# Attention's transposes in unbroken groups, the planner's TensorE spacing, and where attention's output is prepared

## The chip, the cores and the metric

The kernel runs on one core of a Trainium2 chip. The metric is the device time of one execution in microseconds; where several runs are shown, their median counts. The engines are named as the profile names them: PE is TensorE (PEld its weight loads), DVE is VectorE, ACT is ScalarE, POOL is GpSimd, SP is the engine that issues the DMAs.

## The reference

One decoder block on 1024 tokens of width 1024. Half of the mixing width (8 heads of 64) is stick-breaking attention, the other half (4 heads of 128) is a gated DeltaNet in chunks.

```python
h = rmsnorm(x, norm1_w);  proj = h @ w_in
# attention, strictly causal, per head
z = q @ k.T / sqrt(64)
sp = where(causal, softplus(z), 0)
tail = cumsum(sp, reverse=True) - sp
attn = where(causal, exp(log_sigmoid(z) - tail), 0)
o_sb = rmsnorm(attn @ v, sb_norm_w) * silu(sb_z)
# DeltaNet: causal conv + silu on q, k, v, l2norm, chunked delta rule with decay
o_gdn = rmsnorm(gated_delta(q, k, v, decay, beta), gdn_norm_w) * silu(g_z)
x = x + concatenate([o_sb, o_gdn]) @ w_out
return rmsnorm(x, final_norm_w)
```

## The kernel before

Everything is float32. A product that needs full precision is split: each operand into a high part in the format fp32r and a low part, and three matmuls (`mm3`: high x high, high x low, low x high) stand for one. A column of the input projection is 128 outputs wide and takes eight steps (k) of three 512-column matmuls for each half of the tokens. Its weights arrive as `wer`, ScalarE copies them to the high part `weh`, and GpSimd subtracts for the low part `wel` (`Columns.split`, two halves of four k each). The column being computed asks for the split of the next column at its 8th and 12th step.

The program is recorded through a planner. `Model` has a cost for each instruction and keeps a clock; `interleave` runs generators ("streams") and, whenever TensorE's queue in the model is empty, lets the ready stream of the smallest number record its next piece. TensorE's instructions stand in the order in which they were recorded. On the other engines (V, A, G and S for the DMAs) an instruction joins a heap when its inputs are done by the model's clock, and the heap's smallest priority (`ck.prio`, which is a stream's third argument) goes next; this order is then fixed by dependencies. So a cost in the model moves instructions on every engine.

The streams: the DeltaNet ones (load, substitute, solve, pre, scan) come first. Attention follows: `attention` opens a `window` for each head and each quarter of the queries. A window computes scores `z`, two sigmoids, a product scan `cc`, and multiplies them on GpSimd into `sg`. Then it transposes the weights (`st` is the same memory read as fp32r; the profile calls it `stf`) in groups of three or four 128x128 blocks into one PSUM tile, splits that into `ah` and `al`, and multiplies with the values into `po`. At its end it turns two blocks `ot`. `projections` (the columns) is the stream that fills TensorE's gaps. When it is used up, `products_delta` and `products_attention` do so: they multiply the mixed outputs with `w_out`, eight blocks of tokens each, two halves of 12 matmuls per block.

Ahead of the products, `enter_delta` and `enter_attention` load a block `mx` and normalise it, and `prepare` calls `split`, which turns its four 128x128 blocks (plain fp32), multiplies with the gate into `mf`, and makes `mh` (ScalarE) and `ml` (GpSimd). The products' sums are added to the residual `xr` on VectorE; in the last half of each block follow the square sums `sy` (through `yj`), `ry`, the scaling with `fnw` and the write to `out`. `turned` is the helper that records a group of transposes; a yielded `GAP` lets any other ready stream go before this one continues. `ORDER` of the columns, pools and buffer counts are not touched.

All recorded instructions have the line of the recording helper, L360, so the profile tells them apart by the names of their tiles.

Of the kernel before, what the change touches and what calls it, by code (L numbers as in the profile page):

```python
# [11 lines left out]
F32R = mybir.dt.float32r  # L12
I32 = mybir.dt.int32
AF = mybir.ActivationFunctionType
ALU = mybir.AluOpType
# [20 lines left out]
OUT_WEIGHTS, DELTA, WEIGHTS, BANK, WINDOW, OUTPUT, RESULT, DECAYS = -1, 0, 2, 5, 10, 12, 20, 25  # L36
# [6 lines left out]
GAP = "gap"  # L43
# [122 lines left out]
class Model:  # L166
# [3 lines left out]
    def __init__(self, engines):  # L170
        self.now, self.events, self.seq = 0.0, [], 0
        self.regions = {}
        self.heads = {e: [] for e in "VAGS"}
        self.busy = {e: False for e in "VAGS"}
        self.order = {e: [] for e in "VAGS"}
        self.pe, self.pe_busy, self.pe_began, self.table, self.dma = [], False, 0.0, None, 0.0
        self.prio, self.pe_rows, self.pe_words = 0, 128, False

        self.held = {"V": 0.0, "G": 0.0}
        for e, real in engines.items():  # L180
            setattr(self, e, Recorder(self, e, real))
# [18 lines left out]
    def record(self, eng, ins, outs, inputs, cost, table):  # L200
        self.seq += 1
        op = Op(eng, ins, cost, self.prio, self.seq, table)
        if eng == "P":
            op.rows = rows(inputs[0])
            op.words = cost == 58
            op.load = int(np.prod(inputs[0].shape[1:])) * (0.445 if inputs[0].dtype == F32R else 0.834)
        deps = {}
        for ap in outs + inputs:
            r = self.regions.get(ap.tensor.name)
# [112 lines left out]
    def pull(self):  # L322
        if self.pe and not self.pe_busy and not self.pe[0].waits:
            op = self.pe[0]
            self.pe_busy = True
            self.begin(op)
            at = max(self.now, op.ready, self.pe_began + op.load)
            self.pe_began = at

            if op.words and self.pe_words:  # L330
                at += 27
            self.pe_words = op.words
            if op.rows != self.pe_rows:
                at += 150
                self.pe_rows = op.rows
            self.at(at + op.cost, self.pe_done)
# [139 lines left out]
def block(tc, xT_d, x_d, n1_d, wE_d, wQ_d, wC_d, conv_d, alog_d, dtb_d, mixw_d, wo_d, fnw_d, out_d):  # L476
    nc = tc.nc
    ck = Model({"V": nc.vector, "A": nc.scalar, "G": nc.gpsimd, "P": nc.tensor, "S": nc.sync})
    V, A, G, TE, S = ck.V, ck.A, ck.G, ck.P, ck.S

    with ExitStack() as top:
# [69 lines left out]
        def turned(tp, parts):  # L551
            ck.hold(tp)
            for u, a in enumerate(parts):
                if u:
                    yield GAP
                if a.dtype == F32R:
                    TE.transpose(tp[:, u * P:(u + 1) * P].bitcast(F32R), a, idr)
                else:
                    TE.transpose(tp[:, u * P:(u + 1) * P], a, ident)
            ck.free(tp)  # L560

        class Columns:

# [855 lines left out]
        def prepare(g):  # L1419
            for b in range(NB):  # L1420
                yield lambda: ("in", b, g) in ready and (b < 3 or f"{'ad'[g]}{b - 3}" in flags) and (b > 2 or g or f"d{5 + b}" in flags)
                mx, gt, xr, r = ready["in", b, g]
                if g == 0:
                    xr = ready[b, 1][3]
                yield r
                yield lambda: ps.room("pz", 4)
                ready[b, g] = *(yield from split(pools[0], mx, gt)), xr
                yield
# [32 lines left out]
        def enter_attention():  # L1461
            yield lambda: "pool1" in flags and "z3" in flags and 3 in wts
            f0, f1 = pools[0], pools[1]
            for b in range(NB):
                yield lambda: f"e{SBH - 1}{b // 2}" in flags and (b < 3 or (b - 3, 0) in ready)
                mx = f1.tile([P, 512], F32, tag="mx", bufs=3, name="mx")
                gt = f1.tile([P, 4, P], F32, tag="gt", bufs=3, name="gt")
                S.dma_start(mx, o_s[b])
                ck.hold(mx, gt)
                S.dma_start(gt, gate_s[0:4, :, b * P:(b + 1) * P].rearrange("k e t -> e k t"))  # L1470
                o = mx.rearrange("p (h d) -> p h d", d=SBD)
                sq = f0.tile([P, 512], F32, tag="sq", name="sq")
                G.tensor_tensor(sq, mx, mx, ALU.mult)
                ss = f0.tile([P, SBH], F32, tag="ssb", name="ssb")
                V.tensor_reduce(ss, sq.rearrange("p (h d) -> p h d", d=SBD), AX.X, ALU.add)
                rs = f0.tile([P, SBH], F32, tag="rsb", name="rsb")
                V.tensor_scalar(ss, ss, 1.0 / SBD, EPS, ALU.mult, ALU.add)
                rsqrt(rs, ss, SBH)
                ready["in", b, 0] = mx, gt, None, V.tensor_tensor(o, o, rs.unsqueeze(2).to_broadcast([P, SBH, SBD]), ALU.mult)
                yield  # L1480

        def products_attention():
            yield lambda: f"d{NB - 1}" in flags
            for b in range(NB):
# [3 lines left out]
                for got in product(b, 0, parts):  # L1488
# [37 lines left out]
                   [Stream(delta_scan(), 0, DELTA), Stream(delta_solve(), 0.5, DELTA + 0.5), Stream(delta_substitute(), 0.6, DELTA + 0.6),  # L1526
                    pre, Stream(delta_load(), 0.4, DELTA + 0.4), Stream(attention(), 9.995, WINDOW), Stream(attention_values(), 9.99, WINDOW), Stream(out_weights(), 9, OUT_WEIGHTS), fill,
                    Stream(enter_delta(), 9.3, OUTPUT), Stream(prepare(1), 9.2, OUTPUT), Stream(products_delta(), 101, OUTPUT),
                    Stream(enter_attention(), 9.1, OUTPUT), Stream(prepare(0), 9.05, OUTPUT - 1), Stream(products_attention(), 102, OUTPUT - 1.5)])

        order = mybir.DependencyInfo(mybir.DependencyClass.NoSync, mybir.DependencyReason.DATA)
        for ops in ck.order.values():
# [35 lines left out]
```

## Time and profile before

| | us |
|---|---|
| median of 3 runs | 660.68 (659.98 to 661.3) |
| the profiled execution's own time | 661.59 |
| its span | 659.87 |
| TensorE busy in it | 647.9 |
| VectorE, ScalarE, GpSimd busy | 453.9, 382.6, 343.6 |

The span runs from the first to the last instruction. Busy time of TensorE counts from a matmul's start to a modelled end, and neighbouring matmuls overlap, so the distance from start to start is the better measure of what one costs.

### The profile page before, as it was taken

What the parts mean: (1) busy time and instruction counts of PE and PEld (TensorE: products, weight loads), DVE (VectorE), ACT (ScalarE), POOL (GpSimd) and SP (SyncE); (2) the same over time, 40 slices, a digit from 0 to 9 for tenths busy, and PEclk for the clock granted to TensorE, in tenths of its full rate; (3) what the DMA queues carried; (4) which work ended last, traced back from release to release, by engine and by line L of the source; (5) the groups of instructions that cost most, each with busy time, mean ns of one, the idle gap of its engine ahead of it and who ended that gap; (6) DMA issues with size and microseconds to landing.
All of it is one profiled execution on the core that took longest, in us unless ns stands there. A gap on an engine that the chain in (4) does not pass through costs nothing.

```text
span 659.9 us, 11679 instructions
## 1 busy us (share of the span) xinstructions
PE 647.9 (98%) x3978; PEld 553.6 (84%) x3978; DVE 453.9 (69%) x851; ACT 382.6 (58%) x913; POOL 343.6 (52%) x372
## 2 busy tenths in 40 slices
PE   8999999999999999999998999999999999999996
PEld 7889888988878888888887888889888888888885
DVE  4358984434465868776887686775856867868874
ACT  6645567834546776677774576755767577311322
POOL 0106144928674867457858574632533454156753
PEclk9999999999999999999998999999999999999998
DMA  8929336863683353535387253351446916663322
GB/s 297 332 95 364 112 128 224 306 203 112 211 255 134 94 175 110 162 99 180 104 231 230 83 192 100 81 172 61 133 151 198 344 45 224 233 187 96 128 96 96
DMA packets 97643, 111.83 MB, mean 169 GB/s; under 512 B 29552, under 2 KB 62512, under 8 KB 97584
## 3 DMA queue, kind: packets, MB, share of 16 engines
q1 hardware_dynamic: 97584, 111.09, 52.0%
q8 instruction: 31, 0.51, 0.3%
q14 instruction: 28, 0.23, 0.1%
HBM read 76.03 MB, written 35.03 MB: 168 GB/s over the span
## 4 chain that ended last, share of the span: by engine, by line
PE 79%; DMA 8%; DVE 5%; POOL 4%; issue 2%; ACT 1%; SPq 0%; POOLq 0%; ACTq 0%
PE pp L360 50%; PE pz L360 22%; PE po L360 6%; PE pc L360 2%; DMA xr<-xT 2%; DVE xl L360 2%; POOL tt L360 2%; DVE xr L360 2%; DMA rs_s<-rstd 2%; DMA conv<-conv 1%; DMA xr<-x 1%; DMA wcr<-wC 1%; DMA wer<-wE 1%; POOL wel L360 1%; SPq L360 0%
## 5 line engine op out<-in xcount | busy, mean ns | idle before, releaser
L360 PE MATMUL pp<-xh,weh 128*128 128x512 f32 x360 | 152.0, 422 | 0.0
L360 PE MATMUL pp<-xh,wel 128*128 128x512 f32 x360 | 142.0, 395 | 2.4 <-POOL wel L360 2.4
L360 PE MATMUL pp<-xl,weh 128*128 128x512 f32 x360 | 141.6, 393 | 0.5 <-DVE xl L360 0.3
L360 POOL TENSOR_TENSOR sgf<-sgf,cc 128x128 f32<-128x128 f32 (+3 forms) x64 | 79.2, 1238 | 89.6 <-DVE cc L360 61.7
L360 POOL TENSOR_TENSOR wel<-wer,weh 128x512 fp32r<-128x512 f32 x48 | 62.8, 1311 | 51.6 <-ACT weh L360 45.6
L360 PEld LDWEIGHTS pp<-xh,wel 128*128 128x128 f32 x360 | 67.8, 188 | 18.5 <-POOL wel L360 3.2
L360 PEld LDWEIGHTS pp<-xh,weh 128*128 128x128 f32 x360 | 67.8, 188 | 9.7
L360 PEld LDWEIGHTS pp<-xl,weh 128*128 128x128 f32 x360 | 68.2, 189 | 8.7 <-DVE xl L360 1.3
L360 DVE TENSOR_TENSOR al<-pz,ah 128x512 fp32r<-128x512 f32 (+1 forms) x80 | 50.5, 633 | 24.9 <-ACT ah L360 24.4
L360 ACT ACTIVATE sgf<-pz,rs 128x384 f32<-128x384 f32 (+3 forms) x96 | 54.4, 588 | 22.4 <-PE pz L360 21.9
L360 ACT ACTIVATE ah<-pz 128x512 fp32r<-128x512 f32 (+1 forms) x80 | 44.5, 557 | 37.8 <-PE pz L360 37.7
L360 PE MATMUL pz<-step,stf 128*128 128x128 f32 x288 | 60.7, 247 | 0.0
L360 DVE TENSOR_TENSOR_SCAN cc<-pz,step 128x384 f32<-128x384 f32 (+2 forms) x64 | 54.0, 849 | 9.1 <-ACT pz L360 8.5
L360 PE MATMUL pp<-woh,mh 128*128 128x512 f32 (+2 forms) x132 | 52.9, 401 | 0.2 <-DVE xr L360 0.2
L360 ACT ACTIVATE pz<-pz,ns 128x384 f32<-128x384 f32 (+3 forms) x96 | 52.4, 565 | 0.0
L360 PE MATMUL pp<-woh,ml 128*128 128x512 f32 (+2 forms) x132 | 50.9, 385 | 0.0
L360 PE MATMUL pp<-wol,mh 128*128 128x512 f32 (+2 forms) x132 | 50.7, 384 | 0.0
L360 POOL TENSOR_TENSOR ac<-ac,pre 128x512 f32<-128x512 f32 x24 | 31.0, 1290 | 33.5 <-ACT pre L360 16.9
L360 DVE SCALAR_TENSOR_TENSOR pp<-pre,conv,pp 128x512 f32<-128x512 f32 x42 | 31.5, 751 | 23.5 <-ACT pp L360 22.9
L360 PEld LDWEIGHTS pz<-step,stf 128*128 128x128 f32 x288 | 38.8, 141 | 5.8 <-issue 0.2
L360 PE MATMUL po<-ah,v2a 128*128 128x256 f32 (+1 forms) x160 | 42.8, 290 | 0.0
L360 DVE TENSOR_TENSOR_SCAN cc<-pz,cc,step 128x512 f32<-128x512 f32 (+1 forms) x32 | 38.8, 1213 | 4.3 <-ACT pz L360 3.2
(266 smaller groups left out, 1613.2 us busy)
## 6 DMA issues: line engine op xcount, KB each, us to landing
wer<-wE SPq DMA_DIRECT2D x48, 256.0 KB, 3.6
xr<-x SPq DMA_DIRECT2D x16, 512.0 KB, 7.4
g_s<-ac SPq DMA_DIRECT2D x24, 256.0 KB, 2.5
v_s<-v2e SPq DMA_DIRECT2D x16, 256.0 KB, 2.8
kq<-g_s SPq DMA_DIRECT2D x16, 256.0 KB, 4.6
v2a<-v_s SPq DMA_DIRECT2D x8, 512.0 KB, 4.3
q<-qk_s SPq DMA_DIRECT2D x8, 512.0 KB, 3.9
kh<-qk_s SPq DMA_DIRECT2D x8, 512.0 KB, 4.8
```

Source lines behind the costliest of these rows:

```text
L360: ins = f(*args, **kw).ins
```

## The change

The helper `turned` no longer yields between the transposes of a group, so they are recorded one right behind the other. In the model, the extra 27 ns between two transposes of fp32r data are gone; instead the least distance from the start before it (`op.load`) is 0.665 ns per column for such a transpose (85 ns for 128) and 0.845 for any other matmul's weights (108 ns), where it was 0.445 for all fp32r operands (57 ns) and 0.834 for others. The squares of attention's output block go from GpSimd to ScalarE. `enter_attention` gets the priority 9 (OUTPUT - 3) in place of 12 on the queues of V, A, G and S, and `prepare(0)` gets 10 in place of 11; `products_attention` stays at 10.5.

```diff
-            op.words = cost == 58
-            op.load = int(np.prod(inputs[0].shape[1:])) * (0.445 if inputs[0].dtype == F32R else 0.834)
+            op.load = int(np.prod(inputs[0].shape[1:])) * (0.665 if cost == 58 else 0.845)
...
             at = max(self.now, op.ready, self.pe_began + op.load)
             self.pe_began = at
-
-            if op.words and self.pe_words:
-                at += 27
-            self.pe_words = op.words
...
             for u, a in enumerate(parts):
-                if u:
-                    yield GAP
                 if a.dtype == F32R:
                     TE.transpose(tp[:, u * P:(u + 1) * P].bitcast(F32R), a, idr)
                 else:
                     TE.transpose(tp[:, u * P:(u + 1) * P], a, ident)
             ck.free(tp)
+            yield from ()
...
                 sq = f0.tile([P, 512], F32, tag="sq", name="sq")
-                G.tensor_tensor(sq, mx, mx, ALU.mult)
+                A.activation(sq, mx, AF.Square)
...
-                    Stream(enter_attention(), 9.1, OUTPUT), Stream(prepare(0), 9.05, OUTPUT - 1), Stream(products_attention(), 102, OUTPUT - 1.5)])
+                    Stream(enter_attention(), 9.1, OUTPUT - 3), Stream(prepare(0), 9.05, OUTPUT - 2), Stream(products_attention(), 102, OUTPUT - 1.5)])
```

What this moves is shown at three places. The first is TensorE at the first transposes of head 0's last window (15 blocks in four groups); `weh`, `wel` and `pp` belong to a column, `xct`, `v`, `kn`, `at` to the DeltaNet. Before:

```order
L360 MATMUL pz<-step,stf_2684 128x128
L360 MATMUL pp<-xh,weh 128x512
L360 MATMUL pp<-xl,weh 128x512
L360 MATMUL pp<-xh,wel 128x512
L360 MATMUL pc<-xct,xinv 128x128
L360 MATMUL pz<-step,stf_2684 128x128
L360 MATMUL pp<-xh,weh 128x512
L360 MATMUL pp<-xl,weh 128x512
L360 MATMUL pp<-xh,wel 128x512
```

Now, for the same window:

```order
L355 MATMUL pp<-xh,wel 128x512
L355 MATMUL pz<-v_2620,kn 128x128
L355 MATMUL pz<-vr,at 128x128
L355 MATMUL pz<-step,stf_2643 128x128 x8
L355 MATMUL pp<-xh,weh 128x512
L355 MATMUL pp<-xl,weh 128x512
L355 MATMUL pp<-xh,wel 128x512
L355 MATMUL pc<-state,kq 128x128
L355 MATMUL pp<-xh,weh 128x512
L355 MATMUL pp<-xl,weh 128x512
```

Two groups of four stand behind each other as eight transposes, where single ones alternated with a step of a column. Over the whole order, the 384 transposes of fp32r data (`stf`, `otf`, `vt`) form 251 unbroken runs before and 104 now.

The second place is GpSimd around the low weights of the sixteenth column (k3), beside the DeltaNet's third head: `tt` are products of its block solve, `kq` its scaled queries, `sgf` attention's product of sigmoid and scan, `ac` a gate of the convolution. Before:

```order
L360 TENSOR_TENSOR sgf_4045<-sgf_4045,cc 128x896
L360 TENSOR_TENSOR kq<-kq,cb 128x4x128
L360 TENSOR_TENSOR tt<-xa,nb 128x512 x2
L360 TENSOR_TENSOR tt<-yx,xb 128x512 x2
L360 TENSOR_TENSOR wel<-wer,weh 128x512
L360 TENSOR_TENSOR rr<-ss,half 128x8
L360 TENSOR_TENSOR wel<-wer,weh 128x512
L360 TENSOR_TENSOR sgf_4045<-sgf_4045,cc 128x1024
```

Now:

```order
L355 TENSOR_TENSOR ac<-ac,pre 128x512
L355 TENSOR_TENSOR sgf_4289<-sgf_4289,cc 128x1024
L355 TENSOR_TENSOR ac<-ac,pre 128x512
L355 TENSOR_TENSOR wel<-wer,weh 128x512
L355 TENSOR_TENSOR kq<-kq,cb 128x4x128
L355 TENSOR_TENSOR tt<-xa,nb 128x512 x2
L355 TENSOR_TENSOR tt<-yx,xb 128x512
L355 TENSOR_TENSOR wel<-wer,weh 128x512
L355 TENSOR_TENSOR tt<-yx,xb 128x512
L355 TENSOR_TENSOR rr<-ss,half 128x8
```

The column's first `wel` stood behind `kq` and all four `tt` and now stands ahead of them; its second stands behind three of the `tt`.

The third place is VectorE at the last preparation of attention's output: `mx_7628` is the last block's tile, `ssb` and `rsb` its sums and factors, and the additions are `xr<-pp,xr`. Before:

```order
L360 TENSOR_TENSOR xr_6928<-pp_7727,xr_6928 128x512
L360 TENSOR_REDUCE ssb_7634<-sq_7632 128x8
L360 TENSOR_TENSOR mf_7756<-pz_7748,gt_7568 128x512
L360 TENSOR_SCALAR ssb_7634<-ssb_7634 128x8
L360 TENSOR_TENSOR xr_6928<-pp_7744,xr_6928 128x512
L360 SCALAR_TENSOR_TENSOR sy_7740<-sy_7740 128x1
L360 TENSOR_TENSOR mx_7628<-mx_7628,rsb_7636 128x512
L360 SCALAR_TENSOR_TENSOR xr_6928<-xr_6928,ry_7772,fnw_7231 128x1024
L360 TENSOR_TENSOR xr_6938<-pp_7776,xr_6938 128x512
```

Now:

```order
L355 TENSOR_SCALAR ssb_7634<-ssb_7634 128x8
L355 SCALAR_TENSOR_TENSOR xr_6871<-xr_6871,ry_7613,fnw_7309 128x1024
L355 TENSOR_TENSOR xr_6881<-pp_7657,xr_6881 128x512
L355 TENSOR_TENSOR xr_7064<-pp_7689,xr_7064 128x512
L355 SCALAR_TENSOR_TENSOR sy_7653<-sy_7653 128x1
L355 TENSOR_TENSOR mx_7628<-mx_7628,rsb_7636 128x512
L355 SCALAR_TENSOR_TENSOR xr_6881<-xr_6881,ry_7674,fnw_7309 128x1024
L355 TENSOR_TENSOR mf_7732<-pz_7727,gt_7568 128x512
L355 TENSOR_TENSOR xr_7064<-pp_7706,xr_7064 128x512
```

The multiplication that prepares the last block stood behind the additions of the fifth block (`xr_6928`) and now stands behind those of the third (`xr_6881`) and one of the fourth (`xr_7064`).

More of the change, by code (lines that the diff above doesn't have):

```diff
@@ L176, in __init__ @@
         self.pe, self.pe_busy, self.pe_began, self.table, self.dma = [], False, 0.0, None, 0.0
-        self.prio, self.pe_rows, self.pe_words = 0, 128, False
+        self.prio, self.pe_rows = 0, 128
         self.held = {"V": 0.0, "G": 0.0}
```

## The prediction

> **What bounds the kernel now.** I read the page's engine shares first, then its chain, then a table of stretches, and last the timeline of TensorE around transposes and around its longest wait.
>
> ```profile
> PE 647.9 (98%) x3978; PEld 553.6 (84%) x3978; DVE 453.9 (69%) x851; ACT 382.6 (58%) x913; POOL 343.6 (52%) x372
> PE 79%; DMA 8%; DVE 5%; POOL 4%; issue 2%; ACT 1%; SPq 0%; POOLq 0%; ACTq 0%
> 208.00:573.00 365.00, 362.88 (x2415) 311.45 (x2415) 272.08 (x519) 243.07 (x616) 202.66 (x229) 1.00 0.49 154
> 573.00:654.00 81.00, 80.48 (x390) 66.55 (x388) 60.51 (x91) 20.93 (x48) 46.53 (x37) 1.00 0.37 121
> ```
>
> TensorE is busy for 98% of the span and carries 79% of the chain that ended last. The two lower rows are the stretch with attention (208 to 573 us) and the stretch with only output products (573 to 654). Their columns after the length are busy time of PE, PEld, DVE, ACT and POOL, then granted clock. In both, TensorE is never free for long: 362.88 of 365 and 80.48 of 81 us. So time is won by taking TensorE's own time away or by removing one of its few waits, and lost by a new wait. VectorE stands at 272.08 / 365 = 75% beside attention, GpSimd at 56%.
>
> **Part 1: unbroken transposes.** A busy mean of a matmul says little, since they overlap; I go by starts. Column one is the start in us.
>
> ```profile
> 343.73 0.46 PE L360 MATMUL pz<-step,vt 128*128 128x128 f32 x4
> 344.02 0.46 PE L360 MATMUL pp<-xh,weh 128*128 128x512 f32 x1
> 344.32 0.39 PE L360 MATMUL pp<-xl,weh 128*128 128x512 f32 x1
> ...
> 569.38 0.22 PE L360 MATMUL pz<-step,stf 128*128 128x128 f32 x1
> 569.44 0.44 PE L360 MATMUL pp<-woh,mh 128*128 128x512 f32 x1
> 569.73 0.40 PE L360 MATMUL pp<-wol,mh 128*128 128x512 f32 x1
> ...
> 570.19 0.39 PE L360 MATMUL pp<-woh,mh 128*128 128x512 f32 x1
> 570.42 0.39 PE L360 MATMUL pp<-wol,mh 128*128 128x512 f32 x1
> ...
> 570.87 0.29 PE L360 MATMUL pz<-step,stf 128*128 128x128 f32 x2
> 571.00 0.46 PE L360 MATMUL pp<-woh,mh 128*128 128x512 f32 x1
> 571.29 0.39 PE L360 MATMUL pp<-wol,mh 128*128 128x512 f32 x1
> ```
>
> Undisturbed 512-column matmuls start 0.23 us apart (570.19, 570.42). A lone transpose at 569.38 is followed by a matmul 0.06 later, but that matmul needs 0.29 until the next one starts. From the transpose to the second matmul's start it is 0.35, less the ordinary 0.23: **one alone costs 0.12**. Two in a row: 571.29 - 570.87 - 0.23 = 0.19. Four in a row (`vt`, which the kernel never broke up): 344.32 - 343.73 - 0.23 = 0.36. Four alone are 4 x 0.12 = 0.48, two pairs 0.38. So a break costs (0.48 - 0.36) / 3 = 0.04 by the one comparison and 0.02 by the other. I take 0.03.
>
> ```profile
> L360 PE MATMUL pz<-step,stf 128*128 128x128 f32 x288 | 60.7, 247 | 0.0
> L360 PE MATMUL pz<-step,otf 128*128 128x128 f32 x64 | 10.7, 249 | 0.1
> L360 PE MATMUL pz<-step,vt 128*128 128x128 f32 x32 | 4.7, 269 | 0.1
> ```
>
> These are all 288 + 64 + 32 = 384 transposes of fp32r data; only `stf` (attention's weights) goes through the changed helper. Counted in TensorE's order, they stand in 251 unbroken runs before and in 104 now: 147 breaks fewer. TensorE is the bound where they lie, so the term counts in full: **147 x 0.03 = 4.4 us less**, between 147 x 0.02 = 2.9 and 147 x 0.04 = 5.9.
>
> The helper also turns the 64 blocks of `mx`, which are plain fp32.
>
> ```profile
> 576.35 0.60 PE L360 MATMUL pz<-step,mx 128*128 128x128 f32 x4
> 576.70 0.48 PE L360 MATMUL pp<-woh,mh 128*128 128x512 f32 x1
> 577.02 0.39 PE L360 MATMUL pp<-wol,mh 128*128 128x512 f32 x1
> ...
> 633.22 0.38 PE L360 MATMUL pz<-step,mx 128*128 128x128 f32 x2
> 633.36 0.48 PE L360 MATMUL pp<-woh,mh 128*128 128x512 f32 x1
> 633.67 0.39 PE L360 MATMUL pp<-wol,mh 128*128 128x512 f32 x1
> ```
>
> Four cost 577.02 - 576.35 - 0.23 = 0.44, two 0.22: 0.11 each, broken or not. This part is worth nothing.
>
> **Part 2: the new order.** The planner's spacings change, so from the first transposes of `vt` on all engines are ordered anew. On TensorE the same work stands in other places: the last `stf` transpose is matmul 3173 of 3564 before and 2946 now. Attention is finished while column products are still left, and the output products no longer serve as its cover. TensorE's work is the same, so this alone costs nothing. What it can change is the waits. There is one large one.
>
> ```profile
> L360 PE MATMUL pp<-xh,wel 128*128 128x512 f32 x360 | 142.0, 395 | 2.4 <-POOL wel L360 2.4
> L360 PE MATMUL pp<-xl,weh 128*128 128x512 f32 x360 | 141.6, 393 | 0.5 <-DVE xl L360 0.3
> 343.36 0.64 ACT L360 ACTIVATE weh<-wer 128x512 fp32r<-128x512 f32 x1
> 343.25 1.77 POOL L360 TENSOR_TENSOR sgf<-sgf,cc 128x896 f32<-128x896 f32 x1 [0.56 <-DVE cc L360]
> 344.98 1.29 POOL L360 TENSOR_TENSOR kq<-kq,cb 128x512 f32<-128x512 f32 x1
> 346.23 3.12 POOL L360 TENSOR_TENSOR tt<-xa,nb 128x512 f32<-128x512 f32 x2
> 349.32 3.04 POOL L360 TENSOR_TENSOR tt<-yx,xb 128x512 f32<-128x512 f32 x2
> 352.32 1.26 POOL L360 TENSOR_TENSOR wel<-wer,weh 128x512 fp32r<-128x512 f32 x1
> 353.64 0.50 PE L360 MATMUL pp<-xh,wel 128*128 128x512 f32 x1 [1.92 <-POOL wel L360]
> 353.70:359.00 5.30, 5.30 (x22) 4.46 (x23) 4.18 (x5) 0.79 (x2) 4.68 (x3) 0.68 0.85 259
> ```
>
> `wel`, the low part of a column's weights, could have started when `weh` was done, at 344.00. In GpSimd's order it stood behind `sgf`, `kq` and four products `tt`, and began at 352.32. TensorE waited **1.92 us**. The last row, of the stretch behind the wait, has a granted clock of 0.68, so (1 - 0.68) x 5.30 = **1.7 us** more were lost. The wait's price is 3.6 us. In the order now, this column's first `wel` stands ahead of `kq` and the `tt`, so this wait goes. But its second `wel` stands behind `kq` and three `tt`, which are 1.29 + 3 x 1.55 = 5.9 us; it is used four steps (12 matmuls x 0.23 = 2.8 us and what lies between) after the first. So what is late next may be that one. Between 0 and 3.6 us of the wait may come back; I take the half: **1.8 us less**.
>
> The Trainium skill, "TensorE: Matmul & The Clock Gate", Part 1, has the clock fall back only after about 3.4 us of idleness. By that rule this wait would cost 1.92 alone, and its half 1.0, not 1.8. The trace disagrees: 0.68 behind a wait of 1.92.
>
> **Part 3: squares on ScalarE, preparation ahead of the additions.**
>
> ```profile
> L360 POOL TENSOR_TENSOR sq<-mx x8: 1032/1041/2019, 586.0 to 626.1; 128x512 f32<-128x512 f32 x8
> L360 DVE TENSOR_REDUCE ssb<-sq x8: 671/678/686, 587.0 to 634.6; 128x8 f32<-128x512 f32 x8
> L360 DVE TENSOR_TENSOR mx<-mx,rsb x8: 683/1105/1774, 590.5 to 637.8; 128x512 f32<-128x512 f32 x8
> 641.17 1.28 DVE L360 TENSOR_TENSOR xr<-pp,xr 128x512 f32<-128x512 f32 x2
> 642.00 0.47 PE L360 MATMUL pp<-woh,mh 128*128 128x512 f32 x1 [0.19 <-DVE xr L360]
> 647.48 0.63 ACT L360 ACTIVATE yj<-xr 128x512 f32<-128x512 f32 x1 [3.45 <-DVE xr L360]
> ```
>
> Eight squares leave GpSimd (8 x 1.04 = 8.3 us of its 46.53 in the last stretch). ScalarE takes them at about 0.63, the time of the square `yj` of the same size: 8 x 0.63 = 5.0 us on top of 20.93 of 81. Neither is the bound, so this is worth 0. If that cover were gone, a square would cost 0.63 in front of a `mh`. The preparation of attention's blocks now goes ahead on VectorE and on SP's queue (two loads per block). What it passes there are the additions, the output scalings and the writes of results; on GpSimd its `rsb` now stands where the squares stood, ahead of some `ml` and `ry`. By then attention has ended in the new order, so no window stands behind it. An addition that finds a reduce (0.68) and a multiplication (up to 1.77) ahead of it is done 0.68 + 1.77 + 0.64 = 3.1 us after its matmuls. Its `pp` buffer is wanted again after one half block, 12 x 0.23 = 2.8 us: at worst 0.3 for each of 16 additions, 5 us in all. At the median 1.11 of the multiplication it is 2.4, under 2.8, so I take 0. The wait of 0.19 at 642.00, behind such a chain, may go.
>
> **The sum.** The profiled execution took 661.59 us (span 659.87, 1.7 outside it); the median of the three runs is 0.9 lower, 660.68. 661.59 - 4.4 - 1.8 = 655.4, and on the median's footing **654.5 us**.
>
> **The rivals.**
>
> *The wait only moves.* One wait of the same price appears for the one that goes. For it: GpSimd's products still stand ahead of the second `wel`. Then 660.68 - 4.4 = 656.3, still faster. Chance 0.20.
>
> *One wait more.* 656.3 + 3.6 = 659.9, within 0.2% (1.3 us, about what a measurement of this kernel can tell from no change). The change would then not bring what it says. Chance 0.09.
>
> *Attention packed too tightly.* The stretch from the first to the last `stf` shrinks from matmuls 1102 to 3173 to 1063 to 2946, by 9%, with the same work on the other engines: VectorE rises from 75% to about 82%, GpSimd from 56% to 61%. Then `wel` and evacuations are late behind attention's work, as at 352.32. From the second additional wait of 3.6 us on the gain is lost: 656.3 + 2 x 3.6 = 663.5, slower. Against it: in 208 to 573 TensorE lacks only 365 - 362.88 = 2.1 us, nearly all of it that one wait, although the planner's spacing was off by a break's cost at each run. Chance 0.17.
>
> *A break hides the load.* A lone transpose is followed after 0.06 us, four take 0.29 to the next start. If only that counted, four alone would take 0.24, and 72 groups' worth of `stf` (288 / 4) would lose 72 x 0.05 = 3.6: 660.68 + 3.6 = 664.3, slower. Against it stands the matmul behind each run, which takes 0.29 to 0.30 in place of 0.23; with it the lone ones are dearer. Chance 0.04. The Trainium skill, on the same page, "Back-to-back issue gap", speaks for this rival: 128 columns come to about 81 ns each in a stream with weight loads and 56 alone. The trace has the 0.06 too, but the page says nothing of the matmul behind.
>
> **How the numbers follow.** The forecast has the remaining chance, 0.50. Forecast and the moved wait make faster 0.70; one wait more makes same 0.09; the last two make slower 0.21. Low end: breaks at 0.04 (5.9), the whole wait (3.6), the 0.19 and the other short waits in the two group rows (2.4 - 1.92 + 0.5 = 1.0) gone: 660.68 - 10.7 = 650.0. High end: it must hold the case within 0.2% and some of the packed case to leave out no more than 2 in 10: breaks at 0.02 and one wait more is 660.68 - 2.9 + 3.6 = 661.4, rounded up to 662.0.
>
> **What would show it.** Right: in the new profile, runs of four `stf` whose first start and the second matmul's lie about 0.59 apart; TensorE's busy time down by about 4 to 5 us; a granted clock of 1.00 through attention; attention's last `stf` well ahead of the output products; no wait on `wel` near the first `tt` of that column. Wrong: idle TensorE time in attention's stretch above 2.1 us with `wel`, `ah` or `al` as releaser and a clock under 1.00 behind it (packed too tightly); waits on `xr` in the last stretch (part 3's cover gone); a TensorE busy time that does not fall although the runs are joined (the break was free).

## The result and the profile after

The changed kernel takes 659.2 us (median of 20 runs) beside 660.88 of the kernel before (20 runs): a ratio of 0.9974, 95% interval 0.9965 to 0.9983. That is 1.7 us less, faster by 0.26%; a second measurement (e14 below, 12 runs) has 0.9986 (0.9972 to 1.0000). The time lies in the range and on the right side, but the forecast was 6.2 us less: three quarters of the gain are missing. In 8 of its 20 runs the mean granted clock is 0.998 and the time 657.4 to 658.5 us, in the other 12 it is 0.995 to 0.996 and 659.1 to 660.8 us. The profiled execution took 659.28 us with a clock of 0.995, its span is 657.5.

The page's shares and chain, then the two stretches of the table by time (busy PE, PEld, DVE, ACT, POOL, then granted clock), and behind them the stretch from the first to the last `stf` transpose, which is shorter now:

```profile
PE 645.3 (98%) x3978; PEld 553.4 (84%) x3978; DVE 453.8 (69%) x851; ACT 387.5 (59%) x921; POOL 332.2 (51%) x364
PE 87%; DVE 8%; ACT 2%; issue 2%; DMA 1%; SPq 0%; POOL 0%; POOLq 0%; ACTq 0%; DVEq 0%
208.00:573.00 365.00, 362.61 (x2504) 313.21 (x2503) 277.50 (x524) 241.91 (x614) 197.52 (x227) 1.00 0.48 152
573.00:654.00 81.00, 77.73 (x371) 63.89 (x369) 56.80 (x91) 26.44 (x57) 38.80 (x30) 1.00 0.37 125
204.90:520.12 315.22, 312.83 (x2273) 271.93 (x2271) 251.83 (x480) 227.98 (x596) 189.25 (x222) 0.99 0.45 138
```

GpSimd has left the chain of waits, and VectorE has grown in it from 5% to 8%. From 208 to 573 us there are 2504 matmuls where there were 2415, with the same busy time of TensorE. But attention no longer fills that stretch: its transposes lie from 204.90 to 520.12 us, where they lay from 207.97 to 572.47. In these 315 us VectorE is busy for 251.83 / 315.22 = 80%, before for 75%, and GpSimd for 60%, before for 56%. Even so, an average over 315 us hides what happened; the timeline of TensorE shows it. First a run of four between 512-column matmuls, then the place of the new wait (start, length, what it does, idle time before it and what ended that):

```profile
409.23 0.45 PE L355 MATMUL pz<-step,stf 128*128 128x128 f32 x4
409.53 0.47 PE L355 MATMUL pp<-xh,weh 128*128 128x512 f32 x1
409.83 0.40 PE L355 MATMUL pp<-xl,weh 128*128 128x512 f32 x1
...
259.58 0.54 PE L355 MATMUL pz<-step,stf 128*128 128x128 f32 x4
261.08 0.49 PE L355 MATMUL pz<-v,kn 128*128 128x128 f32 x2 [0.96 <-DVE al L355]
262.00 0.79 PE L355 MATMUL pz<-state,kq 128*128 128x128 f32 x2 [0.44 <-DVE state L355]
262.88 0.77 PE L355 MATMUL pp<-xh,weh 128*128 128x512 f32 x1
263.45 0.63 PE L355 MATMUL pp<-xl,weh 128*128 128x512 f32 x1
263.88 0.63 PE L355 MATMUL pp<-xh,wel 128*128 128x512 f32 x1
```

Four transposes cost 409.83 - 409.23 - 0.23 = 0.37, as forecast (0.36). At 260 TensorE stands twice, 1.4 us together, and behind that its 512-column matmuls start 0.57 and 0.43 apart instead of 0.23. The wait on `wel` at 352, the one of the kernel before, is gone. Here are VectorE's timeline ahead of the new wait, and three stretches around it in the table by time:

```profile
258.24 1.28 DVE L355 TENSOR_TENSOR_SCAN cc<-pz,cc,step 128x512 f32<-128x512 f32 x1 [0.23 <-ACT pz L355]
259.44 0.32 DVE L355 TENSOR_SCALAR v<-pc,r2k 128x128 f32<-128x128 f32 x1
259.69 0.74 DVE L355 SCALAR_TENSOR_TENSOR pp<-pre,conv,pp 128x512 f32<-128x512 f32 x1
260.34 0.68 DVE L355 TENSOR_TENSOR al<-pz,ah 128x512 fp32r<-128x512 f32 x1
260.94 0.74 DVE L355 SCALAR_TENSOR_TENSOR pp<-pre,conv,pp 128x512 f32<-128x512 f32 x1
261.60 0.35 DVE L355 SCALAR_TENSOR_TENSOR state<-state,egl,pz 128x128 f32<-128x128 f32 x1
...
250.00:262.00 12.00, 10.57 (x67) 8.67 (x65) 11.61 (x22) 8.54 (x20) 9.18 (x7) 1.00 0.42 118
259.00:262.00 3.00, 1.57 (x9) 0.80 (x7) 3.00 (x7) 3.00 (x7) 1.77 (x1) 0.98 1.02 281
262.00:265.40 3.40, 3.40 (x13) 3.11 (x14) 2.77 (x5) 1.99 (x6) 2.41 (x3) 0.51 0.92 295
```

The same first stretch of the kernel before:

```profile
250.00:262.00 12.00, 11.97 (x76) 10.59 (x75) 9.68 (x22) 9.08 (x36) 10.13 (x8) 1.00 0.30 83
```

In that stretch VectorE is now busy for 11.61 of 12 us; `al`, whose end frees the PSUM bank for the next `v,kn`, stands behind a scan and a step of the convolution, and `state` behind a second one. In the kernel before it was busy for 9.68, and TensorE for 11.97. The slow stretch behind it costs (1 - 0.51) x 3.40 = 1.7 us more: the new wait has a price of 3.1, nearly that of the old one (3.6).

The first 110 us differ by up to 3 us between executions of one kernel, by waits on the loads and casts at the start (from the first matmul to the 561st it is 109.5 to 112.9 over the traces below). From the 561st matmul on, up to which all kernels have the same order on TensorE, the traces compare more closely: 541.9 us to the end of the last matmul before, 539.3 after, and 539.5 in a second trace of the changed kernel. The times in the right column below are counted so.

### The profile page after: what moved, and what is told of

The parts are those of the page before. It is cut to its first block, busy times and chain, and to the rows that moved or that the text cites. A ratio compares the mean times of both kernels' runs of the same rounds, so it can differ in the third digit from the quotient of the medians.

```text
span 657.5 us, 11705 instructions
## 1 busy us (share of the span) xinstructions
PE 645.3 (98%) x3978; PEld 553.4 (84%) x3978; DVE 453.8 (69%) x851; ACT 387.5 (59%) x921; POOL 332.2 (51%) x364
## 4 chain that ended last, share of the span: by engine, by line
PE 87%; DVE 8%; ACT 2%; issue 2%; DMA 1%; SPq 0%; POOL 0%; POOLq 0%; ACTq 0%; DVEq 0%
PE pp L355 53%; PE pz L355 25%; PE po L355 6%; PE pc L355 3%; DVE xl L355 2%; DVE xr L355 2%; DVE cc L355 1%; DMA xr<-xT 1%; DVE pp L355 1%; ACT yj L355 0%; DVE al L355 0%; SPq L355 0%; ACT nkv L355 0%; DVE v2e L355 0%; DVE ac L355 0%
## 5 line engine op out<-in xcount | busy, mean ns | idle before, releaser
L355 PE MATMUL pp<-xh,weh 128*128 128x512 f32 x360 | 148.8, 413 | 0.1
L355 POOL TENSOR_TENSOR sgf<-sgf,cc 128x128 f32<-128x128 f32 (+3 forms) x64 | 77.3, 1210 | 72.4 <-DVE cc L355 58.8
L355 POOL TENSOR_TENSOR ml<-mf,mh 128x512 fp32r<-128x512 f32 x16 | 21.5, 1346 | 47.0 <-ACT mh L355 46.9
L355 PE MATMUL po<-al,v2a 128*128 128x256 f32 (+1 forms) x160 | 39.4, 282 | 0.3 <-DVE al L355 0.3
```

The costliest lines, as they stand in the source:

```text
L355: ins = f(*args, **kw).ins
```

## The experiments

| kernel | median, us | ratio to before, 95% | trace from the 561st matmul, us |
|---|---|---|---|
| before | 660.88 | | 541.9 |
| changed | 659.2 | 0.9974 (0.9965 to 0.9983) | 539.3 |
| e1_groups: before, unbroken groups alone | 664.51 | 1.0049 (1.0033 to 1.0065) | 543.5 |
| e2_spacing: before, new spacings alone | 667.08 | 1.0087 (1.0070 to 1.0103) | 547.0 |
| e3_squares: before, part 3 alone | 664.44 | 1.0046 (1.0031 to 1.0062) | 544.0 |
| e4_groups_spacing: changed, without part 3 | 665.69 | 1.0057 (1.0036 to 1.0077) | 545.1 |
| e9_squares_only: changed, old priorities | 659.89 | 0.9969 (0.9955 to 0.9983) | 539.1 |
| e10_priorities_only: changed, squares on GpSimd | 665.7 | 1.0060 (1.0042 to 1.0077) | 543.4 |

Each ratio is to the kernel before as it ran beside that kernel: its median was 661.17 us beside e1 to e4, 660.89 beside e5 to e8, 662.0 beside e9 to e12, and 661.05 beside e13 to e15. So ratios compare better than medians.

**The parts one by one.**

e1 takes the break out of `turned` and leaves all else:

```diff
-                if u:
-                    yield GAP
...
             ck.free(tp)
+            yield from ()
```

> The kernel before with only the breaks between transposes taken out of the helper; spacing, squares and priorities stay. 107 runs of fp32r transposes in place of 251. Theory A (a break costs 0.03 us; the change's gain was eaten by new waits): TensorE's time in transposes falls by 144 x 0.03 = 4.3 us, so about 656.5 plus or minus the waits that this order happens to bring (up to 3.6 each, wait and slow clock); its trace shows a run of four at 0.36 over the ordinary spacing. Theory B (a break is nearly free, the load hides behind the matmul): within 1 us of the kernel before, with no wait in the trace that explains it.

e2 changes the model's distances, with the groups broken as before:

```diff
-            op.load = int(np.prod(inputs[0].shape[1:])) * (0.445 if inputs[0].dtype == F32R else 0.834)
+            op.load = int(np.prod(inputs[0].shape[1:])) * (0.665 if cost == 58 else 0.845)
...
-            if op.words and self.pe_words:
-                at += 27
```

> The kernel before with only the planner's spacing changed; groups stay broken (254 runs). Theory A: no gain from breaks; the time differs from before only by waits that come and go, so between 657 (the 3.6 us of the wait on wel goes and nothing comes) and 664. Theory C (the better spacing is what helped, by fewer waits): about 658 to 659, as fast as the full change.

e3 puts the squares on ScalarE and changes the two priorities; e4 is e1 and e2 together:

```diff
-                G.tensor_tensor(sq, mx, mx, ALU.mult)
+                A.activation(sq, mx, AF.Square)
...
-                    Stream(enter_attention(), 9.1, OUTPUT), Stream(prepare(0), 9.05, OUTPUT - 1), Stream(products_attention(), 102, OUTPUT - 1.5)])
+                    Stream(enter_attention(), 9.1, OUTPUT - 3), Stream(prepare(0), 9.05, OUTPUT - 2), Stream(products_attention(), 102, OUTPUT - 1.5)])
```

> The kernel before with only the squares on ScalarE and the two priorities; TensorE's order is the same up to the last stretch, so the wait on wel stays. Theory A: 0 to -0.4 us (the wait of 0.19 in the last stretch goes). Theory D (preparation ahead of the additions makes TensorE wait for pp): slower by 0.5 to 5 us, with waits on xr in the last stretch.

> The full change without squares and priorities: unbroken groups and the new spacing. Theory A: the same as the full change within 0.5 us (659.2), with the same wait at 260 us. Theory D: clearly faster than the full change, by 1 us or more.

Every part alone is slower than before, by 3.0 to 5.7 us, and so are the first two together; only all three are faster. The parts don't add up: each of them orders the last stretch anew, and each of these four orders has waits there. TensorE's timeline at it, of e1, of e3 (two rows) and of e4, and behind it e4's stretch in the table by time:

```profile
629.05 0.71 PE L360 MATMUL pz<-step,mx 128*128 128x128 f32 x4 [3.48 <-issue]
...
619.68 0.47 PE L360 MATMUL pp<-woh,mh 128*128 128x512 f32 x1 [1.11 <-DVE ssb L360]
632.72 0.47 PE L360 MATMUL pp<-woh,mh 128*128 128x512 f32 x1 [0.97 <-DVE xr L360]
...
630.82 0.63 PE L355 MATMUL pz<-step,mx 128*128 128x128 f32 x4 [3.47 <-issue]
630.80:636.00 5.20, 5.18 (x17) 3.97 (x18) 3.50 (x4) 0.63 (x1) 2.79 (x3) 0.67 0.26 104
```

In e1 and e4 TensorE reaches attention's blocks before their `mx` is prepared (the profile names no releaser for the wait, only `issue`; in e4 the multiplication that makes `mx` starts at 630.02 and takes 0.69, and the transposes start at 630.82). In e3, whose TensorE order is nearly the old one, the additions are late instead: the preparation ahead of them costs 1.1 and 1.0 us there, where the prediction had at worst 0.3 each. e2 has a wait of 1.70 us there, at 601.76, and one of 0.62 on `ml` at 652.97; the rest of its loss is spread over waits of up to 0.63 in attention's stretch.

I also added up what the transposes of fp32r data cost, run by run, from the start before a run to the second start behind it, less the ordinary distances: 43.9 us in 251 runs before, 38.9 in 104 runs after (5.0 less), 38.0 in e1, 43.6 in e2, 43.9 in e3, 38.9 in e4. The level depends on which distances are taken as ordinary: with the median of the same three matmuls without transposes between them, and medians by length of run, it is 41.3 before and 36.0 after, 5.3 less, and the parts lie as here. So this cost goes with the groups and with nothing else.

**A break by itself.** e5 adds 132 transposes of fp32r data to the output products of the changed kernel, each alone; e6 adds the same 132 in 33 runs of four (the last two lines, in place of the one above the dots):

```diff
                     mm3(yp, mh[:, k, :], ml[:, k, :], w[0][:, hs], w[1][:, hs], k == 0, k == 3)
+                    if "junk" not in flags:
+                        flags["junk"] = pc()
+                    TE.transpose(flags["junk"][:, k * P:(k + 1) * P].bitcast(F32R), idr, idr)
...
+                    for u in range(4 if k == 3 else 0):
+                        TE.transpose(flags["junk"][:, u * P:(u + 1) * P].bitcast(F32R), idr, idr)
```

> The changed kernel with 132 extra fp32r transposes of the identity among the output products, one behind each step's three matmuls, written to a PSUM bank that nothing reads. To be compared with the next kernel, which has the same 132 in 33 runs of four. Theory A (a run costs 0.03 to 0.04 us beside 0.085 for each transpose): 132 x 0.12 = 15.8 us more than the changed kernel, so about 675. Theory B (a lone one hides its load): 132 x 0.06 = 7.9 us more, about 667.

> The same 132 extra transposes in 33 runs of four, behind the last step of each half block. Theory A: 33 x 0.37 = 12.2 us more than the changed kernel, about 671.4, and 3.4 us less than with lone ones. Theory B: 33 x 0.29 = 9.6 us more, about 668.8, and 1.7 us more than with lone ones.

e5 took 674.05 us (1.0201, 1.0183 to 1.0220), e6 671.58 (1.0165, 1.0148 to 1.0183). The 99 breaks between them cost 2.5 us, **0.025 each**, and the 33 runs of four 671.58 - 659.2 = 12.4 us, 0.375 each. The intervals of the two ratios leave 0.01 to 0.04 for a break, and both kernels have waits of their own in the last stretch (1.1 us in e5's trace, 2.3 in e6's). By starts one alone costs 0.11 in e5's trace and a run of four 0.36 in e6's, so a break (4 x 0.11 - 0.36) / 3 = 0.03. That a break hides a transpose is refuted.

**The two waits in attention's stretch.** e7 moves `al` and `state` of the changed kernel two places up on VectorE, and `ah` one place on ScalarE. e8 moves the late `wel` of the kernel before five places up on GpSimd. Both leave every other place as it was (`up` takes an engine, a tile's name and the number of places; the first three lines are e7's, the last e8's):

```diff
+        up('A', 'ah_3079', 1)
+        up('V', 'al_3080', 2)
+        up('V', 'state_3110', 2)
...
+        up('G', 'wel_4206', 5)
```

> The changed kernel with three instructions moved up in their engine's order at 258 to 262 us of its trace: the copy ah ahead of a sigmoid on ScalarE (one place), and on VectorE al ahead of the DeltaNet's v and a convolution step (two places) and state ahead of two convolution steps. TensorE's order is the same. Theory A (the new wait at 260 us, 1.7 us idle or late and about 1.6 of slow clock, ate most of the gain): 1.5 to 3.3 us faster than the changed kernel, 656 to 657.7. If the lost gain lies elsewhere: within 0.5 us of it.

> The kernel before with one instruction moved: the sixteenth column's first wel goes five places up in GpSimd's order, ahead of kq and four tt. Theory A (that wait's price is 1.9 to 2.1 idle and 1.4 to 1.7 of slow clock): 3.4 to 3.6 us faster than before. If the wait only moves to what kq and tt feed: within 1 us of before. By the skill's page with the clock falling back only after 3.4 us of idleness: 1.9 to 2.1 faster.

e7 took 660.9 us (1.0001, 0.9989 to 1.0013), 1.7 slower than the changed kernel; e8 659.62 (0.9980, 0.9968 to 0.9991). TensorE's timeline of e7 (three rows) and of e8:

```profile
260.56 0.46 PE L356 MATMUL pz<-v,kn 128*128 128x128 f32 x2 [0.41 <-DVE v L356]
261.46 0.49 PE L356 MATMUL pz<-state,kq 128*128 128x128 f32 x2 [0.44 <-DVE state L356]
263.70 0.79 PE L356 MATMUL pp<-xh,weh 128*128 128x512 f32 x1 [1.53 <-DVE ac L356]
...
349.97 0.28 PE L361 MATMUL pz<-step,stf 128*128 128x128 f32 x1 [0.95 <-ACT nkv L361]
355.09 0.39 PE L361 MATMUL po<-al,v2a 128*128 128x256 f32 x1 [0.87 <-DVE al L361]
```

In e7 the first wait shrinks, but the convolution that was passed (`ac`) is late in its place, and in e7's trace the clock is at 0.50 from 262.98 to 269.81, for 6.8 us; counted from the 561st matmul that trace has 542.0 us against 539.3. In e8 the wait on `wel` is gone, and two others of nearly the same sum (1.82) stand in its place; only the slow clock behind it is gone. The gain is 1.3 us by the ratio; matmul by matmul, which is possible since TensorE's order is the same, e8's trace is 1.5 us ahead of the one before, all of it won between 348 and 360 us. That is about the 1.7 that I had put on the clock. In both kernels, moving the wait's instruction by order alone moved the wait.

To take VectorE's time away instead, e11 cuts two steps of the convolution at that place to 8 of 512 columns, and e12 (once more as e15, beside the changed kernel as e14) has the twelve copies of three columns `pre` done by ScalarE. The order of all else is unchanged in both (the first three lines are e11's; in e12 `halo` is planned on VectorE and issued on ScalarE):

```diff
+            thin = name == "scalar_tensor_tensor" and args[0].tensor.name == "pp_2794"
+            cut = lambda x: x[:, 0:8] if isinstance(x, bass.AP) and x.shape[-1] == 512 else x
+            ins = f(*(map(cut, args) if thin else args), **kw).ins
...
+            f = lambda o, i: self.model.A.real.activation(o, i, AF.Copy)
...
-                    V.tensor_copy(pre[:, 0:3], last[0][:, 512:515])
+                    V.halo(pre[:, 0:3], last[0][:, 512:515])
...
+        for op in [o for o in ck.order["V"] if o.halo]:
+            ck.order["V"].remove(op)
+            ops = ck.order["A"]
+            ops.insert(next(i for i, o in enumerate(ops) if o.at > op.at), op)
```

> The changed kernel with two steps of one column's convolution on VectorE (the two that stand at 259.69 and 260.94) cut from 512 to 8 columns; the planner still counts them in full, so every engine's order is unchanged; part of that column's convolution is left out. Theory 'VectorE is the bound there': 2 x 0.6 = 1.2 us come free ahead of al and state, the waits of 0.96 and 0.44 and the slow clock at 262 to 266 (0.41 x 4 = 1.6 us) go: 2 to 3.3 us less than the changed kernel, about 656.5. Theory 'something else bounds there' (the wait moves, or the clock falls anyway): within 0.5 us of the changed kernel.

> The changed kernel with the twelve copies of three columns (pre, 0.15 to 1.41 us each on VectorE) on ScalarE, at the place where the planner had them begin; all other instructions keep their order. It computes all that the reference asks for. Theory 'VectorE is the bound at 250 to 262': its 0.71 us at 256.98 comes off the lateness of v, al and state, so that the 1.4 us of waits at 261 fall under 0.8, and with them perhaps the slow clock: 656.5 to 658.5. Rival: ScalarE's queue makes the column's evacuation late instead: 659 to 661.

> The changed kernel itself, beside the next run on the same chip: 0.997 of the kernel before.

> The kernel with the twelve copies of three columns on ScalarE once more, beside the changed kernel itself: if it is faster than that, 0.2% (1.3 us) under it as the ratios to the kernel before have it (0.9954 and 0.9974); if that was the spread between chips, within 0.1%. Its trace showed the waits at 260 to 263 unchanged, which speaks for the second.

e11 took 658.41 us (0.9953, 0.9939 to 0.9968), e12 658.81 (0.9954, 0.9940 to 0.9968). TensorE's timeline of e11, VectorE's at `state`, and the stretches ahead of and behind 262.12:

```profile
261.19 0.49 PE L357 MATMUL pz<-v,kn 128*128 128x128 f32 x2 [0.57 <-DVE al L357]
262.12 0.49 PE L357 MATMUL pz<-state,kq 128*128 128x128 f32 x2 [0.44 <-DVE state L357]
261.72 0.35 DVE L357 SCALAR_TENSOR_TENSOR state<-state,egl,pz 128x128 f32<-128x128 f32 x1 [0.45 <-PE pz L357]
259.12:262.12 3.00, 1.96 (x11) 1.14 (x10) 2.52 (x7) 3.00 (x7) 1.77 (x1) 1.00 1.03 262
262.12:265.52 3.40, 3.40 (x23) 3.04 (x24) 3.40 (x6) 2.75 (x8) 2.03 (x3) 1.00 0.99 332
```

One wait shrinks by 0.4 and the clock stays at 1.00. Matmul by matmul (TensorE's order is the same) e11's trace wins 1.7 us on the changed kernel's between 259 and 266 us and has lost 0.5 before that; the ratios make it 0.9974 - 0.9953 = 0.0021, 1.4 us. That is between the theories' figures but on the side of VectorE's time: VectorE's queue is shown to cost about half of the 3.1 us at this place. The second wait stays: in e11 `state` no longer waits for VectorE's queue but for its own input, the matmul before. e12 didn't do what I meant: its waits at this place are unchanged, 0.95 and 0.44, since VectorE stood idle ahead of the scan instead, 0.47 us for TensorE and 0.37 for ScalarE. Beside the changed kernel on one chip it took 659.28 us (0.9964, 0.9949 to 0.9979) and the changed kernel 660.05 (0.9986, 0.9972 to 1.0000). So both times it was the fastest kernel that computes everything, 0.2% under the changed one by the ratios, with intervals that overlap a little. Counted from the 561st matmul its traces have 539.2 and 538.5 against 539.3 and 539.5. Matmul by matmul they show where a gain lies: each of the two wins 0.24 us at 310 us and 0.54 at 363 to 365 us on either trace of the changed kernel, 0.8 us or 0.12%. The second place is just behind the longest of the copies, 1.41 us at 358.44. Whether it is more than that isn't settled.

**The squares.**

> The changed kernel with the old priorities of attention's output preparation; the squares stay on ScalarE. TensorE's order is that of the changed kernel. Without both (groups and spacing alone) it took 665.7, with both 659.2. Theory 'priorities': the wait of 3.6 us on the mx transposes at 627 came from the loads and from VectorE's and GpSimd's queues; it stays, 664 to 666. Theory 'squares': it came from the square on GpSimd; it goes, 658.5 to 660.

> The changed kernel with the squares back on GpSimd; the new priorities stay. Theory 'priorities': no wait above 1 us at 627, 658.5 to 660.5. Theory 'squares': a wait of 2 to 4 us on the mx transposes late in the last stretch, with a slow clock behind it, 663 to 666. If both halves are needed, this and the run before are both above 662.

e9 and e10 are the changed kernel with one half of part 3 undone (the lines of e3 above). e9 is as fast as the changed kernel, e10 as slow as e4: the priorities are worth nothing that these runs can tell, the squares 5.7 us by the ratios (1.0060 - 0.9974 = 0.0086) and 543.4 - 539.3 = 4.1 by the traces. The reduces of the squares on VectorE in the changed kernel (three rows) and in e10 (four), then three rows of e10's GpSimd and one of its VectorE:

```profile
598.65 0.68 DVE L355 TENSOR_REDUCE ssb<-sq 128x8 f32<-128x512 f32 x1
602.34 0.68 DVE L355 TENSOR_REDUCE ssb<-sq 128x8 f32<-128x512 f32 x1
606.03 0.68 DVE L355 TENSOR_REDUCE ssb<-sq 128x8 f32<-128x512 f32 x1
...
613.49 0.67 DVE L355 TENSOR_REDUCE ssb<-sq 128x8 f32<-128x512 f32 x1
619.18 0.67 DVE L355 TENSOR_REDUCE ssb<-sq 128x8 f32<-128x512 f32 x1
624.56 0.67 DVE L355 TENSOR_REDUCE ssb<-sq 128x8 f32<-128x512 f32 x1
630.87 0.67 DVE L355 TENSOR_REDUCE ssb<-sq 128x8 f32<-128x512 f32 x1
...
619.99 1.04 POOL L355 TENSOR_TENSOR sq<-mx 128x512 f32<-128x512 f32 x1 [1.27 <-DVE ssb L355]
621.20 1.64 POOL L355 TENSOR_TENSOR rsb<-ssb,half 128x8 f32<-128x8 f32 x1 [0.17 <-DVE ssb L355]
622.80 1.29 POOL L355 TENSOR_TENSOR ml<-mf,mh 128x512 fp32r<-128x512 f32 x1
622.87 1.77 DVE L355 TENSOR_TENSOR mx<-mx,rsb 128x512 f32<-128x512 f32 x1 [0.56 <-POOL rsb L355]
```

The steps of the preparation follow each other from VectorE to GpSimd and back: `mx`, the reduce of the block's squares, the next block's square (it waits for that reduce, since there is one `sq` buffer), `rsb`, `mx`. In e10 a turn takes 5.7, 5.4 and 6.3 us (the distances of the reduces), about what TensorE needs for a block (24 matmuls x 0.23 and four transposes at 0.44 in all, 6.0). So the preparation can't get ahead; the last reduce starts at 630.87, where the changed kernel, whose turns begin at 3.7 us, has it at 621.05. The preparation then stands in the way of the additions, and TensorE waits on `xr` for 1.89, 0.57 and 0.52 us. On ScalarE the square no longer stands between the reduce and `rsb` on GpSimd. The multiplication `mx` is longer in e10 too: in seven of its eight turns it begins while `ml` runs on GpSimd and takes 1.46 to 1.77 us, where in five of the changed kernel's eight it begins outside an `ml` and takes 0.68 to 0.69. So a turn of e10 has up to 1.0 us for the square and 1.1 for a slower `mx` more; how far the second follows from the first no run shows.

e13 keeps e10's order on all engines and lets each square compute an eighth of its columns (it takes 0.29 us instead of 1.04):

```diff
+            thin = name == "tensor_tensor" and self.eng == "G" and args[0].tensor.name.startswith("sq_") and args[0].shape[-1] == 512
+            cut = lambda x: x[:, 0:64] if isinstance(x, bass.AP) and x.shape[-1] == 512 else x
+            ins = f(*(map(cut, args) if thin else args), **kw).ins
...
-                V.tensor_reduce(ss, sq.rearrange("p (h d) -> p h d", d=SBD), AX.X, ALU.add)
+                V.tensor_reduce(ss, sq[:, 0:SBD].unsqueeze(1).to_broadcast([P, SBH, SBD]), AX.X, ALU.add)
```

> The changed kernel with the squares on GpSimd as in the run with the new priorities alone (665.7), and in the same order on every engine, but each square computes 64 of its 512 columns (its reduce reads those 64 eight times over, so it takes as long as before; the norm of attention's output is left out so far). Theory 'the square is a link of the loop': mx, reduce, square, rsb and the next mx follow each other from VectorE to GpSimd and back, and 8 x 0.8 us less on GpSimd lets the preparation keep ahead of TensorE: the waits on xr of 1.89, 0.57 and 0.52 shrink under 0.5, 659 to 662. Theory 'the order on GpSimd's queue' (the square waits there for the reduce before it and holds up what stands behind it, however short it is): 664 to 666.

It took 662.76 us (1.0019, 1.0006 to 1.0033). TensorE's timeline:

```profile
620.55 0.50 PE L357 MATMUL pp<-woh,mh 128*128 128x512 f32 x1 [0.52 <-DVE xr L357]
627.49 0.50 PE L357 MATMUL pp<-woh,mh 128*128 128x512 f32 x1 [0.73 <-DVE xr L357]
```

The wait of 1.89 shrinks to 0.73, those of 0.57 and 0.52 stay, and 2.7 of e10's 5.7 us (1.0060 to 1.0019, against 0.9974) are won; by the traces it is 1.3 of 4.1 (543.4 to 542.0, against 539.3). It falls between the theories: a third to a half of the squares' worth is their time in the loop. For the rest their place in GpSimd's queue and the slower `mx` (at the median 1.08 us in e13) are left, which no run shows by themselves.

## Why the prediction was right and wrong

- **Part 1, right.** Forecast 4.4 us less for 147 breaks at 0.03 (2.9 to 5.9). The trace has 5.0 less, the measurement of breaks alone 147 x 0.025 = 3.7. Reading the cost of a run from starts, with the matmul behind it, held; the rival that a break hides a transpose fell. TensorE's busy time went down by 647.9 - 645.3 = 2.6 us, less than the sign of 4 to 5: it counts the slow matmuls behind waits, too. The distances that the Trainium skill's page "TensorE: Matmul & The Clock Gate", "Back-to-back issue gap", gives, and that spoke for this rival, say nothing of the matmul behind a transpose.
- **Part 2, the step that failed: "between 0 and 3.6 us of the wait may come back; I take the half".** The wait on `wel` went. But 3.1 us came back at one place, 260 to 265 us, and by starts another 2.8 in six places of 0.3 to 0.8 us (298, 352, 362, 392, 432 and 618 us). With the transposes: -5.0 - 3.4 (the old wait by starts) + 3.1 + 2.8 = -2.5, and the traces have 539.3 - 541.9 = -2.6 (the medians 1.7 less). The mechanism is that of the rival "attention packed too tightly", at about the price of one wait and some small ones instead of two. I had weighed it by VectorE's mean over attention's stretch, 75% to about 82%. That mean came out nearly as foreseen, 80% (and GpSimd's at 60%, foreseen 61%), and it leaves a fifth of the time free; but VectorE was full where it mattered, 11.61 of 12 us: the new order hands it scans, `al` and a column's convolution at once. That the mean had room said nothing of that place. e4 has the same two waits there and e1, with unbroken groups but the old spacing, hasn't, so they come with the order that both together make. e11 shows by experiment that VectorE's time there costs about 1.7 us; the six small places stand by the accounting of the traces alone, and their sum depends on which distances are taken as ordinary. The places in TensorE's order that the prediction gave (1102 to 3173 of 3564, now 1063 to 2946) differ from the traces', which have 3978 matmuls and attention's transposes from the 1177th to the 3588th before and from the 1090th to the 3361st now: 6% fewer matmuls, but 14% less time (364.5 to 315.2 us).
- **Part 3, a term at 0 that was 5.5 us.** I had it at 0 and took ScalarE's and GpSimd's free time as the cover. It costs 3.0 us on the old order (e3) and wins 5.5 on the new one (e4 against the changed kernel, 1.0057 - 0.9974). That the sum did not miss by as much is luck: the new order brought a wait in the last stretch that part 2 had not counted (3.47 us in e4), and the squares took it away. GpSimd was 52% busy on the whole, but the square was a link of a loop between two engines whose turn was about as long as TensorE's block. The step that failed is "neither is the bound". Without this edit the change would have been slower than before: the order of part 2 needs it.
- **The clock.** The price of a wait as idle time and slow clock behind it was the right way for the waits of the two traces compared: in e8 the clock's part is all that was won, and in e11 most of it. But the clock's part isn't paid each time, as the last section shows, so a price read from one execution can be off by 1.7 us.

## What to carry to other kernels

Weigh a tighter order by the busiest 10 us of each helping engine around the place that moves, not by its mean over the stage: 80% hid a stretch of 97%. An instruction on an engine that is half idle still sets the time where it is a link of a loop between two engines; compare the loop's turn with the time that the bound engine takes for one round. And test the parts of a change on the final order: three edits that each lose alone may win together, and both waits that were attacked by order alone moved by a few us. And where two kernels have the same order on one engine, compare their traces instruction by instruction: that finds 0.2 us where the medians can't.

## What the runs showed of the hardware

The granted clock can fall behind short waits, and then the loss is much the same each time: (1 - 0.68) x 5.30 in the kernel before, (1 - 0.51) x 3.40 in the changed one and (1 - 0.67) x 5.20 in e4 are all 1.7 us, and e7's (1 - 0.50) x 6.83 is twice that. All eight traces with the pair of waits of 0.95 and 0.44 at 260 us have this fall; TensorE is busy for 1.46 to 1.58 of 3 us there. But the share of idle time does not decide it alone. In e10 TensorE was busy for only 1.56 of 3.41 us around the wait of 1.89, and the clock stayed at 1.00; so it did behind e2's wait of 1.70 and e6's of 1.54. It also stayed where TensorE was busy for 1.96 of 3 us (e11) and for 2.05 and 2.21 (e8). Rows of the table by time: e10's wait and the stretch behind it, then the first of e8's.

```profile
625.14:628.55 3.41, 1.56 (x9) 0.95 (x7) 3.41 (x6) 0.58 (x1) 3.02 (x2) 1.00 0.37 153
628.55:631.97 3.42, 3.38 (x15) 2.81 (x16) 3.35 (x5) 1.50 (x5) 2.13 (x3) 1.00 0.01 1
...
349.00:352.00 3.00, 2.05 (x12) 1.68 (x12) 2.52 (x6) 1.66 (x10) 3.00 (x3) 1.00 0.95 348
```

Nor does one kernel have the fall in every execution: 1.7 us lost of 657.5 put the mean clock at 0.9974 at best, and 8 of the changed kernel's 20 executions have 0.998. What decides it, no run here shows. The Trainium skill, "TensorE: Matmul & The Clock Gate", Part 1, has the clock fall after an idle window of about 3.4 us, and in the same part reports a kernel in which short idle times between groups of matmuls made it oscillate; here waits of 1.4 us within 3 us were enough in eight traces and one of 1.92 in two (before, e3), while one of 1.89 in e10 was not.

A copy of three columns takes from 0.15 to 1.41 us on VectorE, and a steady 0.19 on ScalarE. In the changed kernel's trace the four copies beside which GpSimd computes nothing take 0.15 to 0.16 us; the other eight end within 0.03 us of the end of the GpSimd instruction that ran when they began. The two lists are duration min/median/max in ns, of the changed kernel and of e12; the last two rows are the longest copy and the GpSimd instruction beside it:

```profile
L355 DVE COPY pre<-pre x12: 147/496/1414, 87.9 to 358.4; 128x3 f32<-128x3 f32 x12
L354 ACT ACTIVATE pre<-pre x12: 187/193/237, 85.9 to 358.5; 128x3 f32<-128x3 f32 x12
...
357.82 2.01 POOL L355 TENSOR_TENSOR sgf<-sgf,cc 128x1024 f32<-128x1024 f32 x1 [1.49 <-DVE cc L355]
358.44 1.41 DVE L355 COPY pre<-pre 128x3 f32<-128x3 f32 x1
```
